# Alternating rooms for the first words of the Strassen blocks, and half of one weight sum moved from transfers to VectorE

## The chip, the cores and the metric

The kernel runs on one core of a Trainium2 chip. The time is the device time of one execution in microseconds (us). Three executions of the kernel before took 964.87, 967.33 and 967.99 us; the median is 967.33 us. One more execution was recorded by the hardware profiler and took 968.38 us, of which the first to the last instruction (the span) is 966.3 us; the other 2.1 us lie around it.

The engines are PE (TensorE, matrix products; PEld is its loading of the stationary operand), DVE (VectorE), ACT (ScalarE), POOL (GpSimd) and SP (SyncE, which here only issues loads). Sixteen DMA engines carry out the transfers. The tensors lie in HBM, the working tiles in SBUF, and the results of the matrix products in PSUM.

## The reference, cut to what matters

An encoder of two layers works on 256 tokens of width 1024 in float32. Each layer has an FFN, a mixer (mLSTM in layer 0, windowed attention in layer 1) and a second FFN, with a layer norm behind each. So there are six stages: FFN, mLSTM, FFN, FFN, attention, FFN. The change touches the four FFNs.

```python
D_MODEL, SEQ, DEPTH, D_FF = 1024, 256, 2, 2816
def swiglu(x, w_in, w_out):                 # w_in 1024 x 5632, w_out 2816 x 1024
    gu = x @ w_in
    g, u = gu[..., :D_FF], gu[..., D_FF:]
    return (jax.nn.silu(g) * u) @ w_out
# in each layer
x = layer_norm(ALPHA * x + 0.5 * swiglu(x, ffn_w_in[l, 0], ffn_w_out[l, 0]), ...)
y = mlstm_mixer(x, ...) if l % 2 == 0 else window_attention(x, ...)
x = layer_norm(ALPHA * x + y, ...)
x = layer_norm(ALPHA * x + 0.5 * swiglu(x, ffn_w_in[l, 1], ffn_w_out[l, 1]), ...)
```

## The kernel before

**Words and splits.** Every weight is used once, and it comes from HBM as a *word*: a tile of 128 x 1024 float32 (512 KB). A word is *split* into a high part, which ACT casts (`high`, tile `w_hi`), and a low part, the rest, which DVE subtracts (`low`, tile `w_lo`). A product of float32 accuracy is then three matmuls: high by high, high by low, low by high (`mm3`). PE needs both parts of a word; ten of each can be there at a time (`RING`), so the splits can run ahead of the products.

**Rooms.** A raw word lies in a *room*, a buffer of a pool, until its last low part or last sum is done (`drop`); then `load` issues the next word's transfer on SP. `w_raw` has 4 rooms and serves all stages. Within an FFN there are 2 spare rooms for the same words (`v_raw`, `V_RAW = 2`) and three kinds with 2 rooms each, `s_raw0` to `s_raw2`, for the Strassen blocks. The profile names a tile by its kind of word: `w_raw` (also in a spare room) or `s_raw`.

**A Strassen block** (`seven` in the plan, `seven` in `ffn`) makes 512 gate and 512 up columns of the FFN's hidden layer with seven products of blocks where eight would be due. The weights of a block are four quarters, of two words each: first (gate columns, upper rows; `b11`), second (up columns, upper rows; `b12`), third (gate columns, lower rows) and fourth (up columns, lower rows; `b22`). The words of `b11` are added to in place and split four times. The plan of one block, in the order in which the words are split, is:

- `s1`: the two words of `b11` as loaded. Behind each, `b11 += b12` on DVE, and `b12 +=` fourth quarter by an *accumulating transfer*: POOL issues a DMA that adds from HBM onto the tile (`sum`, line 272).
- the two words of the third quarter (`piece`), then one word of the output matrix (a *down* word).
- `s5`: `b11` again (now first + second). Behind each, `b11 += b22` on DVE. Then a second down word.
- `s6`: `b11` again. Behind each, `b11 +=` third quarter by an accumulating transfer.
- the two words of `b12` (second + fourth), the two of `b22`, two more down words, and last `b11` once more. This last pair of splits is called *s4* below. In the fourth block of an FFN the two late down words are left out.

So a block needs four sums on DVE and four accumulating transfers of 512 KB. A block's three kinds of rooms rotate: `TAGS[1 + (r + n) % 3]` gives the next block's `b11` the rooms of this block's `b12`, its `b12` those of `b22`, and its `b22` those of `b11`. An FFN has four blocks (`SEVENS = 4`), before them fourteen words and behind them six down words.

**The order in time.** Nothing is scheduled by the chip: each engine works off its instructions in the order in which the program wrote them, and waits at each for what it needs. The program decides the order while it is built, with a model of the engines' clocks (`Paced`). Within an FFN, after each matmul, `fill` writes a high part, a low part or a sum as soon as the model says that the engine is free and that the data have been there for 1 us (`SOON`). For a load the model counts `LANDING` and `LOADING`, for an accumulating transfer 8 us from its issue (`ADDING`). A product whose words are not yet split makes `take` write all splits of the plan up to them. The `turn` of a split gives the order in which PE takes it, where that differs from the order of splitting.

Between the products stand small steps on DVE and ACT. Two matter here: `end3` (a subtraction and a multiplication on DVE, 128 x 512, tile `e`), which makes the hidden values of the first 128 tokens, and `tr` behind it, four transposes by PE of that tile (`pw<-ident,e` in the profile), one down word later. The pair of `end3` is called *the e pair* below. The place where one block's late products meet the next block's first words is called *the border*.

Of the kernel before, what the change touches and what calls it, by code (L numbers as in the profile page):

```python
# [9 lines left out]
F32 = mybir.dt.float32  # L10
# [6 lines left out]
D = 1024  # L17
# [4 lines left out]
F = 2816  # L22
UNITS = F // 256
SEVENS = 4
RAW_BUFS = 4
S_RAW = 2
TAGS = ("w_raw", "s_raw0", "s_raw1", "s_raw2")
V_RAW = 2
RING = 10
PU = [2, 0, 1, 2, 1, 2, 1, 1, 0, 1, 2, 4]  # L30
QC = [2, 12, 20, 28, 32]
# [15 lines left out]
LANDING = 2200.0  # L47
LOADING = 1340.0
SECOND = 1250.0
ADDING = 8000.0  # L50


class Paced:
# [94 lines left out]
class Weights:  # L148
# [5 lines left out]
    def __init__(self, nc, pool, words, plan, after, turns):  # L154
# [4 lines left out]
        self.order, self.left = turns, set(range(len(plan)))  # L159
        self.todo = {tag: [i for i, w in enumerate(words) if w["tag"] == tag] for tag in TAGS}  # L160
        self.free = {"v_raw": 0, **{tag: 0 for tag in TAGS}, "w_raw": RAW_BUFS}
        self.spool, self.send, self.vbufs = None, 0, 0
# [13 lines left out]

    def open(self, pool, end, s_raw=S_RAW, v_raw=V_RAW):

# [84 lines left out]
    def sum(self):  # L263
        nc = self.nc
        _, w, v = self.sums.pop(0)
        t = self.raw[w]
        if isinstance(v, int):
            nc.vector.tensor_add(t, t, self.raw[v])
            self.drop(v)
            self.load()  # L270
        else:
            nc.gpsimd.dma_start(t.rearrange("p (k f) -> p k f", k=self.words[w]["k"]), v, accum_op=OP.add)  # L272
            nc.mark(t, max(nc.vec, nc.pe) + ADDING)

    def fill(self):

# [52 lines left out]
def trunk_kernel(ctx: ExitStack, tc: tile.TileContext, x, ffn_w_in, ffn_w_out, ln_g, ln_b, ml_w_in, ml_gate_b,  # L329
                 ml_norm_g, ml_w_out, at_w_in, at_sink, at_w_out, out):  # L330
    nc = Paced(tc.nc)
# [9 lines left out]
    words, plan, after = [], [], {}  # L341

    def word(src, k, tag="w_raw"):
        words.append(dict(src=src, k=k, tag=tag))
        return len(words) - 1

    def split_of(w, scale=None, needs=None):

        plan.append(dict(word=w, k=words[w]["k"], scale=scale, needs=needs, turn=len(plan)))
        return len(plan) - 1  # L350
# [4 lines left out]
    def two(w, r0, c0):  # L355
        return w[r0:r0 + 256, c0:c0 + 512].rearrange("(k p) f -> p k f", p=128)
# [12 lines left out]
    def rows(w, c, scale=None):  # L369
        piece(w[c * 128:(c + 1) * 128, :].rearrange("(k p) f -> p k f", p=128), 1, scale)  # L370

    def seven(w, c0, c1, n, downs):

        at = lambda r0, c: [two(w, r0 + 256 * j, c) for j in range(2)]
        b12, b11, b22 = ([word(x, 2, TAGS[1 + (r + n) % 3]) for x in at(*p)]
                         for r, p in ((1, (0, c1)), (0, (0, c0)), (2, (512, c1))))
        s1 = [split_of(w_) for w_ in b11]
        for a in at(512, c0):
            piece(a, 2)
        for j, a in enumerate(at(512, c1)):  # L380
            after[s1[j]] = [(b11[j], b12[j]), (b12[j], a)]
        downs(0)
        s5 = [split_of(w_, None, p) for w_, p in zip(b11, s1)]
        downs(1)
        for j in range(2):
            after[s5[j]] = [(b11[j], b22[j])]
        s6 = [split_of(w_, None, p) for w_, p in zip(b11, s5)]
        for j, a in enumerate(at(512, c0)):
            after[s6[j]] = [(b11[j], a)]
        plan[s6[0] - 1]["turn"] += 2.5  # L390
        [split_of(w_, None, p) for w_, p in zip(b12, s1)]
        for w_ in b22:
            split_of(w_)
        downs(2)
        downs(3)
        [split_of(w_, None, p) for w_, p in zip(b11, s6)]
        if n < SEVENS - 1:
            plan[-3]["turn"] += 2.5

    ends = {}  # L400
    for j, (kind, l, i, _) in enumerate(stages):
        if kind == "ffn":
            wi, wo = ffn_w_in[l, i], ffn_w_out[l, i]
            nth = iter(range(2 * UNITS))

            def down(n):
                for _ in range(n):
                    rows(wo, next(nth))

            for c0 in (0, F):  # L410
                for a in range(4):
                    wide(wi, a * 256, c0)
            for a in range(4):
                beside(wi, a * 256, 512, F + 512)
            down(2)
            for g in range(SEVENS):
                c0 = 768 + 512 * g
                seven(wi, c0, F + c0, g, lambda i_: down(1) if g < SEVENS - 1 or i_ < 2 else None)
            down(6)
        elif kind == "mlstm":  # L420
            for c0 in (1024, 1536):
                for a in range(4):
                    wide(ml_w_in[0], a * 256, c0)
            for c0 in range(0, 1024, 256):
                for a in range(2):
                    narrow(ml_w_in[0], a * 512, c0)
            for c0 in (2048, 2560):
                for a in range(4):
                    wide(ml_w_in[0], a * 256, c0)
            for c in range(8):  # L430
                rows(ml_w_out[0], c, (lambda c=c: gcol[:, c:c + 1]))
        else:
            for c0 in (1024, 0):
                for a in range(4):
                    wide(at_w_in[0], a * 256, c0)
            for c0 in (512, 768):
                for a in range(2):
                    narrow(at_w_in[0], a * 512, c0)
            for c in range(8):
                rows(at_w_out[0], c)  # L440
        ends[j] = len(words)
# [87 lines left out]
    def load_ln(room, l, n):  # L529
        t = []  # L530
        for name, w in (("g", ln_g), ("b", ln_b)):
            a = room("ln_" + name)
            src = w[l, n]
            nc.sync.dma_start(a, bass.AP(tensor=src.tensor, offset=src.offset, ap=[[0, 128], [1, D]]))
            t.append(a)
        return t
# [89 lines left out]
    def ffn(l, i, n, pending, last):  # L626
        with ExitStack() as ph:
            pool = ph.enter_context(tc.tile_pool(name="ffn", bufs=1))
# [140 lines left out]
            def down(n_):  # L769
                if not y:  # L770
                    y.extend([ybank() for _ in range(2)] for _ in range(2))
                for _ in range(n_):
                    c = done_[0]
                    w, = W.take(1)
                    for t in range(2):
                        for o in range(2):
                            mm3(y[t][o], pair(hT[c], A, tok(t)), pair(w, A, 0, slice(o * 512, o * 512 + 512)),
                                c == 0, False)
                    W.done()
                    done_[0] += 1  # L780
# [96 lines left out]
            def turn():  # L877
                p = wbank((128, 2, S))
                for t in range(2):
                    for k in range(2):  # L880
                        nc.tensor.transpose(p[:, k, tok(t)], hh[t][:, k * 128:(k + 1) * 128], ident)
                split_evac(hp, p)

            down(1)
            for g in range(SEVENS):
                turn = seven(g < SEVENS - 1, turn)
            if start:
                small_loads()
            nc.filler = None
            gb = load_ln(lambda name: pool.tile([128, D], F32, name=name, tag=TAGS[1 + SEVENS % 3], bufs=S_RAW), l, n)  # L890
            norm = [Norm(t, 2 * ALPHA, 4 * LN_EPS, gb, last) for t in range(2)]
            todo = list(zip(range(2 * UNITS - 6, 2 * UNITS), W.take_rows(6)))
            W.done(0)
# [510 lines left out]
    for j, (kind, l, i, n) in enumerate(stages):  # L1404
        last = j == len(stages) - 1
# [37 lines left out]
```

## Time and profile before

| what | value |
|---|---|
| three executions | 964.87, 967.33, 967.99 us |
| the profiled execution | 968.38 us, span 966.3 us |
| mean granted clock of TensorE | 0.984 |
| transfers | 208.53 MB in the span, mean 216 GB/s |
| busy share of PE, DVE, ACT, POOL | 95, 84, 59, 16% |
| `s_raw` loads on SP | 96, median 8.6 us from issue to landing |
| accumulating transfers on POOL | 64, median 6.8 us from issue to landing |

The page of the profile gives for each engine the busy time and the number of instructions. A row of a group of instructions ends in two parts behind bars: the busy time with the mean duration of one (ns), and the time that the engine stood idle just before them with what ended the idling. A row of the timeline gives start and length in us, engine, line, operation, output and inputs, the shape, the number of instructions that follow each other without a break, and in brackets the idle time before with what ended it. A row of the windows gives, for a stretch of the span, the busy time of each engine, the granted clock of TensorE (PEclk, 1.00 is full), the busy share of the sixteen DMA engines (which can come out a little above 1) and the GB/s. A row of the waits says who waited for whom: us in total, how often, and the longest.

### The profile page before, as it was taken

The numbers are of one execution on the slowest core, as the hardware profiler recorded it, in microseconds if no ns is written. First come the engines' busy times: TensorE is split into PE (matmuls) and PEld (weight loads), VectorE is DVE, ScalarE is ACT, GpSimd is POOL, SyncE is SP. The second block draws the span as 40 slices with busy tenths as digits, with TensorE's granted clock in tenths as the row PEclk, the third lists the DMA queues.
The fourth block names the chain that finished last, engine by engine and source line by source line (L and its number), as shares of the span: only waits on it lengthen the run. The fifth ranks groups of instructions, "written<-read, shape, count | busy, mean of one in ns | idle before, by whom it ended". The sixth has DMA issues, their size and how long they took to land.

```text
span 966.3 us, 12569 instructions
## 1 busy us (share of the span) xinstructions
PE 921.5 (95%) x4459; PEld 764.5 (79%) x4459; DVE 810.0 (84%) x969; ACT 568.3 (59%) x793; POOL 155.2 (16%) x194
## 2 busy tenths in 40 slices
PE   9998899799999999998989999898999999899896
PEld 7887778589988887887778888786888888788775
DVE  5889888787699798988897899887868889899776
ACT  5657565545765566656545676655459566666560
POOL 0012013022321010111011010110345301102010
PEclk9999999999999999998999999999999999999999
DMA  8998998545625979987659789876433387998941
GB/s 279 336 240 246 267 277 188 199 128 166 227 95 183 329 176 295 268 218 242 171 169 347 191 263 301 258 176 200 141 139 131 96 279 236 253 268 223 280 109 44
DMA packets 100702, 208.53 MB, mean 216 GB/s; under 512 B 6904, under 2 KB 21264, under 8 KB 100640
## 3 DMA queue, kind: packets, MB, share of 16 engines
q1 hardware_dynamic: 82368, 173.04, 51.2%
q0 software_dynamic: 17696, 33.65, 20.6%
q10 hardware_dynamic: 576, 1.05, 0.3%
q8 instruction: 35, 0.57, 0.2%
q14 instruction: 27, 0.22, 0.1%
HBM read 206.65 MB, written 1.05 MB: 215 GB/s over the span
## 4 chain that ended last, share of the span: by engine, by line
PE 43%; DVE 19%; DMA 15%; issue 15%; ACT 4%; POOL 3%; SPq 0%; DVEq 0%; POOLq 0%; ACTq 0%
PE pw L139 28%; PE py L139 15%; DMA s_raw<-in_ffn_w_in_dram 11%; DVE w_lo L139 9%; ACT w_hi L139 3%; DVE s_raw L139 3%; DVE e L139 2%; POOL s_raw L272 2%; DMA w_raw<-in_ffn_w_out_dram 1%; DMA w_raw<-in_ml_w_in_dram 1%; DMA w_raw<-in_ffn_w_in_dram 1%; DVE h_lo L139 1%; DMA w_raw<-in_at_w_in_dram 1%; DVE x L139 1%; DVE h L139 1%
## 5 line engine op out<-in xcount | busy, mean ns | idle before, releaser
L139 DVE TENSOR_TENSOR w_lo<-w_raw,w_hi 128x1024 fp32r<-128x1024 f32 (+1 forms) x213 | 253.8, 1219 | 28.9 <-ACT w_hi L139 26.8
L139 DVE TENSOR_TENSOR w_lo<-s_raw,w_hi 128x1024 fp32r<-128x1024 f32 x192 | 227.5, 1219 | 52.1 <-ACT w_hi L139 47.8
L139 ACT CAST w_hi<-w_raw 128x1024 fp32r<-128x1024 f32 (+1 forms) x213 | 216.1, 1046 | 69.4 <-PE py L139 22.1
L139 ACT CAST w_hi<-s_raw 128x1024 fp32r<-128x1024 f32 x192 | 191.9, 1051 | 79.4 <-DMA s_raw<-in_ffn_w_in_dram 50.0
L139 PE MATMUL pw<-w_hi,xT_hi 128*128 128x512 f32 x480 | 193.5, 404 | 1.7 <-ACT w_hi L139 1.7
L139 PE MATMUL pw<-w_hi,xT_lo 128*128 128x512 f32 x480 | 189.1, 395 | 0.8 <-DVE xT_lo L139 0.8
L139 PE MATMUL pw<-w_lo,xT_hi 128*128 128x512 f32 x480 | 188.9, 395 | 0.4 <-DVE w_lo L139 0.4
L272 POOL DMA_DIRECT2D s_raw<-in_ffn_w_in_dram x64 | 77.7, 1232 | 519.4 <-ACT w_hi L139 158.5
L139 PE MATMUL py<-w_hi,h_lo 128*128 128x512 f32 x349 | 138.2, 396 | 6.2 <-DVE h_lo L139 6.2
L139 PE MATMUL py<-w_hi,h_hi 128*128 128x512 f32 x349 | 138.6, 397 | 3.4 <-ACT h_hi L139 3.4
L139 PE MATMUL py<-w_lo,h_hi 128*128 128x512 f32 x349 | 138.2, 396 | 2.5 <-DVE w_lo L139 2.5
L139 PEld LDWEIGHTS pw<-w_hi,xT_lo 128*128 128x128 f32 x480 | 91.6, 191 | 21.2 <-DVE xT_lo L139 1.3
L139 PEld LDWEIGHTS pw<-w_hi,xT_hi 128*128 128x128 f32 x480 | 91.6, 191 | 19.6 <-ACT w_hi L139 2.1
L139 PEld LDWEIGHTS pw<-w_lo,xT_hi 128*128 128x128 f32 x480 | 91.9, 191 | 19.0 <-DVE w_lo L139 1.2
L139 PE MATMUL pw<-w_hi,S_hi 128*128 128x512 f32 x256 | 99.6, 389 | 0.0
L139 PE MATMUL pw<-w_lo,S_hi 128*128 128x512 f32 x256 | 99.6, 389 | 0.0
L139 PE MATMUL pw<-w_hi,S_lo 128*128 128x512 f32 x256 | 99.6, 389 | 0.0
L139 PEld LDWEIGHTS py<-w_hi,h_lo 128*128 128x128 f32 x349 | 66.5, 191 | 21.6 <-DVE h_lo L139 7.9
L139 PEld LDWEIGHTS py<-w_lo,h_hi 128*128 128x128 f32 x349 | 66.4, 190 | 19.7 <-DVE w_lo L139 6.4
L139 PEld LDWEIGHTS py<-w_hi,h_hi 128*128 128x128 f32 x349 | 66.7, 191 | 17.8 <-ACT h_hi L139 4.3
L139 DVE TENSOR_TENSOR s_raw<-s_raw,s_raw 128x1024 f32<-128x1024 f32 x64 | 78.3, 1224 | 2.5 <-DMA s_raw<-in_ffn_w_in_dram 0.8
L139 ACT COPY e<-pw 128x512 f32<-128x512 f32 x48 | 28.2, 587 | 61.7 <-PE pw L139 61.7
(205 smaller groups left out, 1157.0 us busy)
## 6 DMA issues: line engine op xcount, KB each, us to landing
s_raw<-in_ffn_w_in_dram SPq DMA_DIRECT2D x96, 512.0 KB, 8.6
w_raw<-in_ffn_w_out_dram SPq DMA_DIRECT2D x88, 512.0 KB, 7.0
w_raw<-in_ffn_w_in_dram SPq DMA_DIRECT2D x64, 512.0 KB, 4.9
s_raw<-in_ffn_w_in_dram POOLq DMA_DIRECT2D x64, 512.0 KB, 6.8
w_raw<-in_ml_w_in_dram SPq DMA_DIRECT2D x24, 512.0 KB, 4.6
w_raw<-in_ffn_w_in_dram SPq DMA_DIRECT2D x32, 256.0 KB, 3.4
w_raw<-in_at_w_in_dram SPq DMA_DIRECT2D x12, 512.0 KB, 4.6
w_raw<-in_ml_w_out_dram SPq DMA_DIRECT2D x8, 512.0 KB, 4.0
```

Of the source, the lines that this page charges most:

```text
L139: r = f(out, *args, **kw)
L272: nc.gpsimd.dma_start(t.rearrange("p (k f) -> p k f", k=self.words[w]["k"]), v, accum_op=OP.add)
```

## The change

Five things change.

1. A fourth kind of room, `s_raw3`, comes in (two rooms), and the spare rooms `v_raw` go from 2 to 1, so an FFN has 13 rooms where it had 12. The rooms no longer rotate: `b12` always has `s_raw1`, `b22` always `s_raw2`, and `b11` has `s_raw0` in even blocks and `s_raw3` in odd ones. The layer norm's two vectors go into `s_raw0`.
2. The last pair s4 of a block is split behind the next block's `s1` (`late`). The order in which PE takes the words stays.
3. The second down word is split behind `s6`, not between `s5` and `s6`.
4. In every FFN but the first (`both` is `j == 0`), for one of the two words of `b12`, the sum of second and fourth quarter is `b12 += b22` on DVE behind `s5`, and the accumulating transfer for it is dropped. For the other word, and in the first FFN for both, the transfer stays. These are 12 transfers fewer of 64 and 12 DVE sums more.
5. In the model of the clocks an accumulating transfer now also takes up the transfers' time: 2500 ns each (`SHARE`), so loads issued behind it count as landing later.

```diff
-TAGS = ("w_raw", "s_raw0", "s_raw1", "s_raw2")
-V_RAW = 2
+TAGS = ("w_raw", "s_raw0", "s_raw1", "s_raw2", "s_raw3")
+V_RAW = 1
...
+SHARE = 2500.0
...
             nc.gpsimd.dma_start(t.rearrange("p (k f) -> p k f", k=self.words[w]["k"]), v, accum_op=OP.add)
-            nc.mark(t, max(nc.vec, nc.pe) + ADDING)
+            now = max(nc.vec, nc.pe)
+            nc.dma = max(nc.dma, now + LANDING) + SHARE
+            nc.mark(t, now + ADDING)
...
-    def seven(w, c0, c1, n, downs):
-        at = lambda r0, c: [two(w, r0 + 256 * j, c) for j in range(2)]
-        b12, b11, b22 = ([word(x, 2, TAGS[1 + (r + n) % 3]) for x in at(*p)]
-                         for r, p in ((1, (0, c1)), (0, (0, c0)), (2, (512, c1))))
+    def seven(w, c0, c1, n, down, late, both):
+        def at(r0, c):
+            return [two(w, r0 + 256 * j, c) for j in range(2)]
+        b12, b11, b22 = ([word(x, 2, TAGS[r]) for x in at(*p)]
+                         for r, p in ((2, (0, c1)), (4 if n % 2 else 1, (0, c0)), (3, (512, c1))))
+        first = len(plan)
+        used = iter(range(99))
+        def turn(n_):
+            for p in plan[-n_:]:
+                p["turn"] = first + 0.01 * next(used)
         s1 = [split_of(w_) for w_ in b11]
+        turn(2)
+        for j, a in enumerate(at(512, c1)):
+            after[s1[j]] = [(b11[j], b12[j])] + [(b12[j], a)] * (j or both)
+        late()
         for a in at(512, c0):
             piece(a, 2)
-        for j, a in enumerate(at(512, c1)):
-            after[s1[j]] = [(b11[j], b12[j]), (b12[j], a)]
-        downs(0)
+        turn(2)
+        down()
+        turn(1)
         s5 = [split_of(w_, None, p) for w_, p in zip(b11, s1)]
-        downs(1)
+        turn(2)
         for j in range(2):
-            after[s5[j]] = [(b11[j], b22[j])]
+            after[s5[j]] = [(b11[j], b22[j])] + [(b12[j], b22[j])] * (not (j or both))
+        full = n < SEVENS - 1
         s6 = [split_of(w_, None, p) for w_, p in zip(b11, s5)]
+        turn(2)
         for j, a in enumerate(at(512, c0)):
             after[s6[j]] = [(b11[j], a)]
-        plan[s6[0] - 1]["turn"] += 2.5
-        [split_of(w_, None, p) for w_, p in zip(b12, s1)]
+        down()
+        turn(1)
+        [split_of(w_, None, p) for w_, p in zip(b12, (s1[0] if both else s5[0], s1[1]))]
+        turn(2)
         for w_ in b22:
             split_of(w_)
-        downs(2)
-        downs(3)
-        [split_of(w_, None, p) for w_, p in zip(b11, s6)]
-        if n < SEVENS - 1:
-            plan[-3]["turn"] += 2.5
+        turn(2)
+        if full:
+            down()
+            turn(1)
+        at4 = [next(used) for _ in range(2)]
+        if full:
+            down()
+            turn(1)
+        def last():
+            for j in range(2):
+                split_of(b11[j], None, s6[j])
+                plan[-1]["turn"] = first + 0.01 * at4[j]
+        return last
...
+            late = lambda: None
             for g in range(SEVENS):
                 c0 = 768 + 512 * g
-                seven(wi, c0, F + c0, g, lambda i_: down(1) if g < SEVENS - 1 or i_ < 2 else None)
+                late = seven(wi, c0, F + c0, g, lambda: down(1), late, j == 0)
+            late()
             down(6)
...
-            gb = load_ln(lambda name: pool.tile([128, D], F32, name=name, tag=TAGS[1 + SEVENS % 3], bufs=S_RAW), l, n)
+            gb = load_ln(lambda name: pool.tile([128, D], F32, name=name, tag=TAGS[1], bufs=S_RAW), l, n)
```

## The prediction

> **What bounds the kernel now.** I read the page first, then the waits of PE, then the timeline where PE waits, then windows over blocks.
>
> ```profile
> span 966.3 us, 12569 instructions
> ...
> PE 921.5 (95%) x4459; PEld 764.5 (79%) x4459; DVE 810.0 (84%) x969; ACT 568.3 (59%) x793; POOL 155.2 (16%) x194
> ```
>
> PE is the bound with 95%, so only its idle time and its slow time can be won. The waits of PE, over the whole span and then over the blocks of the four FFNs in turn (40 to 180 us, 340 to 480, 530 to 665, 805 to 966):
>
> ```profile
> PE pw L139 <- DVE e L139: 20.6, 10, 3.0
> PE pw L139 <- ACT w_hi L139: 1.7, 1, 1.7
> PE py L139 <- DVE w_lo L139: 2.7, 10, 0.9
> ...
> PE pw L139 <- DVE e L139: 7.6, 3, 2.8
> PE pw L139 <- DVE e L139: 3.9, 2, 3.0
> PE pw L139 <- DVE e L139: 3.1, 2, 2.8
> PE pw L139 <- DVE e L139: 6.0, 3, 2.9
> ```
>
> PE hardly waits for split weights (2.7 us for low parts). It waits ten times, 20.6 us, for the e pair: the transposes `tr` at the borders of blocks. Why the pair is late, at the first border (timelines of POOL, SP, DVE, ACT and PE, put in order of time; between them how long the two accumulating transfers took to land, each asked of its own window):
>
> ```profile
> 59.49 2.44 POOL L272 DMA_DIRECT2D s_raw<-in_ffn_w_in_dram  x2 [10.30 <-DVE w_lo L139]
> ...
> DMA to landing us min/median/max: 5.7/5.7/5.7
> ...
> DMA to landing us min/median/max: 10.9/10.9/10.9
> ...
> 61.49 3.78 SPq L105 DMA_DIRECT2D s_raw<-in_ffn_w_in_dram  x4
> 66.03 1.48 SPq L105 DMA_DIRECT2D w_raw<-in_ffn_w_out_dram  x2
> ...
> 67.06 1.22 DVE L139 TENSOR_TENSOR w_lo<-s_raw,w_hi 128x1024 fp32r<-128x1024 f32 x1
> 68.25 0.69 DVE L139 TENSOR_TENSOR e<-e,pw 128x512 f32<-128x512 f32 x1
> ...
> 71.56 2.95 ACT L139 CAST w_hi<-s_raw 128x1024 fp32r<-128x1024 f32 x3 [5.21 <-DMA s_raw<-in_ffn_w_in_dram]
> ...
> 72.65 2.36 DVE L139 TENSOR_TENSOR w_lo<-s_raw,w_hi 128x1024 fp32r<-128x1024 f32 x2 [3.72 <-ACT w_hi L139]
> 74.93 0.69 DVE L139 TENSOR_TENSOR e<-pw,e 128x512 f32<-128x512 f32 x1
> 75.65 0.69 DVE L139 TENSOR_TENSOR e<-e,e 128x512 f32<-128x512 f32 x1
> ...
> 76.49 0.63 PE L139 MATMUL pw<-ident,e 128*128 128x128 f32 x4 [2.84 <-DVE e L139]
> ```
>
> The second transfer for s4 is issued at 60.6 (second of the pair at 59.49) and lands 10.9 us later, at 71.5, beside a burst of loads from 61.49 on. ACT stands 5.21 us before its high part, DVE 3.72 us before its low part, and the e pair, which has all it needs, is written behind that low part. In DVE's order three low parts stand ahead of the pair: 67.06 is the first word of s4, 72.65 (x2) the second of s4 and the first of the next block's `s1`.
>
> The idle stretches cost a second time. The windows behind four of them, one more of the gaps, and then whole blocks:
>
> ```profile
> 143.40:146.90 3.50, 3.50 (x11) 2.91 (x12) 3.50 (x4) 1.53 (x2) 1.20 (x1) 0.51 0.67 242
> 440.30:447.30 7.00, 6.05 (x17) 4.93 (x18) 5.99 (x7) 2.48 (x3) 2.41 (x2) 0.51 0.85 172
> 628.10:631.60 3.50, 3.50 (x11) 2.75 (x10) 3.47 (x5) 2.48 (x3) 1.14 (x1) 0.51 0.90 145
> 904.60:908.10 3.50, 2.97 (x10) 2.58 (x11) 3.46 (x5) 1.85 (x3) 0.98 (x2) 0.51 0.77 170
> ...
> 840.26 0.41 PE L139 MATMUL pw<-ident,e 128*128 128x128 f32 x2 [2.44 <-DVE e L139]
> ...
> 76.90:110.40 33.50, 31.05 (x143) 25.47 (x141) 29.53 (x30) 21.25 (x25) 4.84 (x4) 1.00 0.91 252
> 376.70:407.60 30.90, 30.90 (x144) 25.59 (x142) 28.84 (x29) 20.30 (x24) 4.80 (x4) 1.00 0.91 255
> 563.30:594.20 30.90, 30.90 (x143) 25.59 (x142) 29.01 (x29) 20.31 (x24) 4.82 (x4) 1.00 0.93 260
> ```
>
> In 17.5 us the clock is at 0.51, so 17.5 x 0.49 = 8.6 us are lost. A block of the first FFN takes 33.5 us from border to border, one without a wait 30.9. **The ceiling** is 20.6 + 1.7 + 8.6 = 30.9 us. The two borders without a wait show that the same products need no wait.
>
> **The change part by part.**
>
> *s4 split behind the next `s1`.* Nothing is added; two low parts and two high parts change places with two. Now three low parts stand ahead of the e pair; if as many stand there after, they are two of `s1` and the first of s4, whose transfer landed in 5.7 us. The late second word comes behind the pair and is not missed yet: at the first border it lands at 71.5, plus a high part of 1.05 and a low part of 1.22 makes 73.8, and PE, which without the wait would do `tr` at 76.49 - 2.84 = 73.65 and then the first word of s4, 12 matmuls for two words at the blocks' pace, asks for the second word later than that. For the two low parts of `s1` to run early, their word must be there: in its own room it can be loaded a block ahead, where before it came with the burst at 61.49. Queued behind s4's waiting high part on ACT are the third quarter's high parts and the next casts of evacuations; DVE's queue is what counts, and there the pair is ahead. Bounds of the rest of a wait per border: 0 (the pair is ahead), and 2.84 - 1.22 = 1.6 us (the order against the pair stays as it was, and only the transfer starts one low part earlier, below). I take 0.5, since the blocks of 30.9 us show borders at 0; for 12 borders 6.0 us stay.
>
> *Second down word behind `s6`.* One low part (1.22 us) less ahead of the accumulating transfer, so that starts by as much earlier. Against it, `s6` has one split less to cover its sum on DVE. Rows of the sum and of POOL's issue:
>
> ```profile
> L139 DVE TENSOR_TENSOR s_raw<-s_raw,s_raw 128x1024 f32<-128x1024 f32 x64 | 78.3, 1224 | 2.5 <-DMA s_raw<-in_ffn_w_in_dram 0.8
> L272 POOL DMA_DIRECT2D s_raw<-in_ffn_w_in_dram x64 | 77.7, 1232 | 519.4 <-ACT w_hi L139 158.5
> ```
>
> The second word's low part and sum lie between and cover a cast of 1.05 us. Taken at 0, bounds -1.2 and +1.2 per block, inside the 0.5 above.
>
> *Sums on VectorE for transfers.* Removed: 12 x 1.23 us of issue on POOL (519.4 us idle ahead of it: nothing) and 12 of 64 transfers. Their engine time:
>
> ```profile
> q1 hardware_dynamic: 82368, 173.04, 51.2%
> q0 software_dynamic: 17696, 33.65, 20.6%
> ```
>
> 20.6% of 966.3 us over 64 is 3.1 us each (a load of 512 KB: 51.2% over 173.04 MB, 1.5 us), 37 us of transfers less, which nobody waits for by themselves; it shows in landing times. Added: 12 x 1.224 = 14.7 us on DVE. In a block without waits DVE has 28.84 to 29.01 of 30.9 us; with one sum it has 30.1 to 30.2, so 0.7 us of cover is left, and behind the sum stand the low parts of `s5` and `s6`. Bounds 0 (covered) and 14.7; nearest is the room of 0.7 us, so near 0: I take 2.0.
>
> *Rooms.* Loads keep their number but for their order. At the start of an FFN all `s_raw` rooms fill at once, now eight and not six:
>
> ```profile
> 23.68 0.60 SPq L105 DMA_DIRECT2D w_raw<-in_ffn_w_out_dram  x1
> 24.33 4.80 SPq L105 DMA_DIRECT2D s_raw<-in_ffn_w_in_dram  x6
> 29.24 0.67 SPq L105 DMA_DIRECT2D w_raw<-in_ffn_w_out_dram  x1
> ...
> 40.01 1.05 ACT L139 CAST w_hi<-w_raw 128x1024 fp32r<-128x1024 f32 x1 [1.53 <-DMA w_raw<-in_ffn_w_out_dram]
> ...
> 187.41 1.05 ACT L139 CAST w_hi<-w_raw 128x1024 fp32r<-128x1024 f32 x1 [3.90 <-DMA w_raw<-in_ml_w_in_dram]
> ```
>
> The load at 29.24 moves behind two more, 2 x 1.5 = 3.0 us, and with a spare room less the one at 23.68 comes behind the `s_raw` loads too. ACT already waited 1.53 us for it. Bounds 0 and 4 x 3.0 = 12; PE had no wait of this kind in the windows above, so I take 1.0, in the first FFN. At the end of an FFN a room less for the six down words can hold the next stage's first load back by a word; ACT waits there today (3.90 us). Bounds -2 and +4 (one word of 1.3 us at three boundaries); taken at 0, since the next stage never used the spare rooms.
>
> *`SHARE`.* No instruction; loads count 2.5 us later per accumulating transfer, so splits of late words are written later. This is what keeps the order above; 0 by itself.
>
> **Sum.** 30.9 - 6.0 - 2.0 - 1.0 = 21.9 us off the profiled execution's 968.4 us gives 946.5. The median shown is 1 us below that execution, so I say **946**.
>
> **The clock.** The half clock begins as the gap ends, after gaps of at most 3.0 us, in four of the seven large ones (rival 1). The Trainium skill, "TensorE: Matmul & The Clock Gate", Part 1, says that the clock halves after at least one idle window of about 3.4 us. By that rule no gap here would have done it, and the 8.6 us would stay whatever the gaps do: 955. The rows differ from the rule, so I count the clock with the gaps.
>
> **The rivals.**
>
> *1. The pair stays behind the late word.* The model still writes both words of s4 ahead of the pair. Seven gaps are large: three in the first FFN (7.6), 3.0, 2.8, 2.44 and 2.9; the other three make 20.6 - 18.7 = 1.9 us. Then the large ones lose 1.2 us each (8.5) and the small ones go; half of the clock's 8.6 comes back. 968.4 - 8.5 - 1.9 - 4.3 + 3.0 = 957. For: the model put 8 us on a transfer of 10.9. Against: three splits ahead, now of other words.
>
> *2. VectorE becomes the bound in three FFNs.* All 14.7 us show: 946.5 + 12.7 = 959. For: 0.7 us of cover. Against: DVE's waits of 3.72 us go.
>
> *3. The next block's sum takes the place of the late word (slower).* `b11 += b12` of the next block is now due before s4, and `b12`'s room comes free only in the burst at 61.49; its second load goes at about 62.6. If the model writes this sum ahead of the pair and the load takes 11.4 us, the longest of any `s_raw` transfer, it lands at 74.0, sum 75.2, pair 76.6, where 73.65 was due: 2.9 us at each of 12 borders (35 us), with 1.2 us of clock each (8.6 over seven): 968.4 - 30.9 + 35 + 15 + 3 = 990. It decides from 1.6 us per border with the clock, a landing 10.1 us after issue; the middle is 979. For: loads in the burst share with two transfers. Against: median landing of 8.6 us, and `SHARE`.
>
> ```profile
> s_raw<-in_ffn_w_in_dram SPq DMA_DIRECT2D x96, 512.0 KB, 8.6
> ...
> DMA to landing us min/median/max: 5.6/8.1/11.4
> ```
>
> *4. Nothing moves.* Gaps go and come back elsewhere: 967.
>
> *5. The clock does not come back:* 955, above.
>
> **How the numbers follow.** Forecast 0.55 (938 to 954), rival 1 0.15, rival 2 0.10, rival 5 0.05, rival 3 0.11, rival 4 0.04. Range 936 to 965: all 30.9 won and 1.5 us of better stage ends, up to rivals 1 and 2 with 6 us; it leaves out rivals 3 and 4 and the tails, 0.2. A change of 0.3% (2.9 us) is about what a measurement of this kernel tells from none. Faster 0.85, within 0.3% 0.04, slower 0.11. The forecast's own range is 938 to 954.
>
> **What the profile after would show.** PE's wait for `e` under 7 us and no PEclk of 0.51 behind a border (right) or 10 us and more (rival 1, 3). DVE at a border: two low parts of `s1`, one of s4, the pair, the second of s4. ACT's wait for `s_raw` by transfers below half. 52 accumulating transfers and 76 sums on DVE; blocks of the later FFNs at 31 us (right) or 32 and more with DVE at 97% (rival 2). DVE waiting for a transfer before a sum would be rival 3. A PE wait for low parts near the 40th us of the span or at the ends of FFNs would show the rooms' price. The prediction is wrong if the model's new order puts another late word ahead of the pair.

## The result, and the profile after

Over 20 executions the kernel after takes 970.40 us in the median (964.77 to 974.08). The kernel before, over 20 executions beside them, takes 968.99 us (964.87 to 975.92). The ratio is 1.0009 with a 95% interval of 0.9991 to 1.0028: no difference that this measurement can tell. The forecast of 946 us and its range of 936 to 965 us missed. The profiled execution of after took 970.03 us, with a span of 968.3 us and a mean granted clock of 0.983.

First the page of after: the span, the engines, the queue of the accumulating transfers (packets, MB, share of the sixteen DMA engines), the chain by engine, and the groups of the sums and of the accumulating transfers.

```profile
span 968.3 us, 12517 instructions
...
PE 922.8 (95%) x4459; PEld 765.4 (79%) x4459; DVE 823.1 (85%) x981; ACT 568.6 (59%) x793; POOL 140.6 (15%) x182
...
q0 software_dynamic: 14432, 27.35, 17.0%
...
DVE 37%; PE 26%; DMA 24%; issue 8%; ACT 4%; POOL 1%; SPq 0%; DVEq 0%; ACTq 0%; POOLq 0%
...
L140 DVE TENSOR_TENSOR s_raw<-s_raw,s_raw 128x1024 f32<-128x1024 f32 x76 | 92.0, 1224 | 16.5 <-DMA s_raw<-in_ffn_w_in_dram 14.4
...
L273 POOL DMA_DIRECT2D s_raw<-in_ffn_w_in_dram x52 | 62.9, 1213 | 535.7 <-ACT w_hi L140 222.0
```

The counts are those forecast: 52 accumulating transfers and 76 sums, and the share of the DMA engines that these transfers take falls from 20.6 to 17.0%. PE is as busy as before (922.8 against 921.5 us). What moved is the chain that ended last. The same row of the page of before was:

```profile
PE 43%; DVE 19%; DMA 15%; issue 15%; ACT 4%; POOL 3%; SPq 0%; DVEq 0%; POOLq 0%; ACTq 0%
```

VectorE's part of the chain went from 19 to 37%, the transfers' from 15 to 24%, and PE's fell from 43 to 26%. In the sums' row the idle time ahead of them, spent on a transfer, went from 0.8 to 14.4 us.

The waits of PE in after (us in total, how often, the longest), and below them one row each of the waits of DVE and of ACT:

```profile
PE pw L140 <- DVE e L140: 21.7, 16, 3.7
PE py L140 <- DVE h_lo L140: 5.3, 6, 2.0
PE py L140 <- ACT h_hi L140: 4.5, 2, 3.6
PE pw L140 <- DVE w_lo L140: 3.7, 2, 3.2
```

```profile
DVE s_raw L140 <- DMA s_raw<-in_ffn_w_in_dram: 14.4, 13, 2.2
```

```profile
ACT w_hi L140 <- DMA s_raw<-in_ffn_w_in_dram: 18.4, 12, 2.3
```

In before, ACT's row was:

```profile
ACT w_hi L139 <- DMA s_raw<-in_ffn_w_in_dram: 50.0, 19, 5.3
```

So ACT no longer stands before the late word (50.0 us became 18.4), as forecast. Its waiting has moved, though: for the sums of VectorE ahead of its casts it waited 29.3 us in before (20 times) and waits 65.9 us in after (30 times). And PE's wait for the e pair is as large as it was (20.6 us ten times, now 21.7 us sixteen times), and VectorE now waits for transfers ahead of its sums.

The timeline of DVE over the first border of the second FFN shows both. The last row is PE's, from its own timeline:

```profile
361.19 1.22 DVE L140 TENSOR_TENSOR w_lo<-s_raw,w_hi 128x1024 fp32r<-128x1024 f32 x1
363.79 1.23 DVE L140 TENSOR_TENSOR s_raw<-s_raw,s_raw 128x1024 f32<-128x1024 f32 x1 [1.38 <-DMA s_raw<-in_ffn_w_in_dram]
364.93 1.22 DVE L140 TENSOR_TENSOR w_lo<-s_raw,w_hi 128x1024 fp32r<-128x1024 f32 x1
366.58 1.23 DVE L140 TENSOR_TENSOR s_raw<-s_raw,s_raw 128x1024 f32<-128x1024 f32 x1 [0.43 <-DMA s_raw<-in_ffn_w_in_dram]
367.73 0.68 DVE L140 TENSOR_TENSOR e<-e,pw 128x512 f32<-128x512 f32 x1
368.33 2.35 DVE L140 TENSOR_TENSOR w_lo<-s_raw,w_hi 128x1024 fp32r<-128x1024 f32 x2
370.60 0.68 DVE L140 TENSOR_TENSOR e<-pw,e 128x512 f32<-128x512 f32 x1
371.31 0.69 DVE L140 TENSOR_TENSOR e<-e,e 128x512 f32<-128x512 f32 x1
```

```profile
372.15 1.09 PE L140 MATMUL pw<-ident,e 128*128 128x128 f32 x4 [2.50 <-DVE e L140]
```

The low parts at 361.19 and 364.93 are those of the next block's `s1`. Each is followed by a sum `b11 += b12` of that next block, and VectorE stands 1.38 and 0.43 us before them for the loads of `b12`. Then come both low parts of s4 (368.33, x2), and only then the e pair at 370.60, for which PE idles 2.50 us. The row at 367.73 is an earlier step between the products. The timelines at the other borders show the same at ten of the twelve: all four low parts and both sums stand ahead of the pair. At the first two borders of the first FFN one and three low parts stand there.

Windows over five blocks of the later FFNs, from border to border. The columns are those of the prediction's windows:

```profile
372.20:405.90 33.70, 32.41 (x140) 26.56 (x141) 30.88 (x31) 21.36 (x25) 3.58 (x3) 0.96 0.79 234
405.90:438.60 32.70, 31.08 (x141) 25.50 (x141) 30.88 (x31) 21.26 (x25) 3.61 (x3) 1.00 0.82 241
595.90:627.60 31.70, 31.08 (x141) 25.51 (x141) 30.88 (x31) 21.32 (x25) 3.61 (x3) 1.00 0.82 249
843.70:878.50 34.80, 33.81 (x141) 27.62 (x141) 30.98 (x31) 21.34 (x25) 3.59 (x3) 0.92 0.76 228
878.50:910.90 32.40, 31.03 (x141) 25.48 (x141) 30.84 (x31) 21.26 (x25) 3.61 (x3) 1.00 0.82 244
```

A block has 31 instructions of VectorE and 30.8 to 31.0 us of its work, and it takes 31.7 to 34.8 us. VectorE has as much to do in it as PE has in a block without a wait (30.9 us). By stage, from the last transposes ahead of an FFN's blocks (`pw<-ident,hh`) to the `tr` of its fourth block, read from the starts of those rows in the timeline of PE (us):

| FFN | before | after |
|---|---|---|
| first | 124.6 | 126.8 |
| second | 122.0 | 123.5 |
| third | 120.0 | 122.6 |
| fourth | 124.8 | 125.2 |

No FFN got shorter: together they take 6.8 us more. Something else got shorter, by 7.9 us: the stretch from the end of the first FFN's blocks to the start of the second's, with the mLSTM in it, takes 177.1 us in before and 169.2 in after. In before (176 to 350 us) PE waits there for 5.2 us, and its clock is low behind these waits:

```profile
PE py L139 <- DVE h_lo L139: 2.0, 1, 2.0
PE py L139 <- ACT h_hi L139: 1.7, 1, 1.7
PE py L139 <- DVE w_lo L139: 1.5, 4, 0.9
...
186.00:200.00 14.00, 10.31 (x34) 7.72 (x33) 9.59 (x12) 3.63 (x4) 1.55 (x1) 0.76 0.51 173
```

In after, 0.6 us of such waits are left. SP issues the mLSTM's first four loads together there, from 174.70 us on; in before two go out at 176.15 and the next at 179.70. No run tests this gain by itself. It takes rooms and order together: the stretch is 179.6 us with the rooms alone and 176.4 us with the order alone (both runs below).

### The profile page after: what moved, and what is told of

Its sections match the earlier page's. It is cut to its first block, busy times and chain, and to the rows that moved or that the text cites. A ratio compares the mean times of both kernels' runs of the same rounds, so it can differ in the third digit from the quotient of the medians.

```text
span 968.3 us, 12517 instructions
## 1 busy us (share of the span) xinstructions
PE 922.8 (95%) x4459; PEld 765.4 (79%) x4459; DVE 823.1 (85%) x981; ACT 568.6 (59%) x793; POOL 140.6 (15%) x182
## 4 chain that ended last, share of the span: by engine, by line
DVE 37%; PE 26%; DMA 24%; issue 8%; ACT 4%; POOL 1%; SPq 0%; DVEq 0%; ACTq 0%; POOLq 0%
DVE w_lo L140 21%; PE pw L140 17%; DMA s_raw<-in_ffn_w_in_dram 15%; PE py L140 8%; DMA w_raw<-in_ffn_w_in_dram 4%; DVE e L140 4%; DVE s_raw L140 4%; DMA w_raw<-in_ffn_w_out_dram 3%; ACT w_hi L140 2%; DVE h_lo L140 2%; DVE x L140 2%; DVE stats L140 1%; DMA w_raw<-in_at_w_in_dram 1%; DMA w_raw<-in_ml_w_in_dram 1%; DVE h L140 1%
## 5 line engine op out<-in xcount | busy, mean ns | idle before, releaser
L140 ACT CAST w_hi<-s_raw 128x1024 fp32r<-128x1024 f32 x192 | 194.3, 1049 | 88.4 <-DVE s_raw L140 65.9
L273 POOL DMA_DIRECT2D s_raw<-in_ffn_w_in_dram x52 | 62.9, 1213 | 535.7 <-ACT w_hi L140 222.0
L140 DVE TENSOR_TENSOR s_raw<-s_raw,s_raw 128x1024 f32<-128x1024 f32 x76 | 92.0, 1224 | 16.5 <-DMA s_raw<-in_ffn_w_in_dram 14.4
L140 PEld LDWEIGHTS py<-w_hi,h_lo 128*128 128x128 f32 x349 | 66.3, 190 | 21.7 <-DVE h_lo L140 7.8
L140 PEld LDWEIGHTS py<-w_hi,h_hi 128*128 128x128 f32 x349 | 66.5, 191 | 19.1 <-ACT h_hi L140 5.3
L140 ACT CAST h_hi<-pw 128x512 fp32r<-128x512 f32 x44 | 25.8, 588 | 66.6 <-PE pw L140 66.5
```

Of the source, the lines that this page charges most:

```text
L140: r = f(out, *args, **kw)
```

## The experiments

Two theories stood against each other. V says that VectorE's own time is what the gain went into: the 12 sums leave it no slack. Q says that it is the place in VectorE's queue: the next block's sums and low parts stand ahead of the e pair and wait for loads. A third reading, D, puts it down to the data, that is when transfers and loads land. Each experiment has its theories' numbers as they were recorded.

### VectorE's time

**All by transfer.** After, with item 4 of the change taken back:

```diff
-                late = seven(wi, c0, F + c0, g, lambda: down(1), late, j == 0)
+                late = seven(wi, c0, F + c0, g, lambda: down(1), late, True)
```

> The kernel after, with the sum of second and fourth quarter by accumulating transfers for both words in all FFNs (64 transfers and 64 sums on VectorE as before); rooms and order as after. Theory V: 8 to 14 us faster than after. Theory Q: the next block's sums still stand ahead of the pair, so within 4 us of after, PE's wait for e 17 to 27 us.

Measured: 948.48 us, 0.9781 of before (0.9753 to 0.9808). That is 22 us less than after, for 12 sums of 1.22 us (14.7 us). Of 19.1 us between the two profiled spans (968.3 and 949.2), 10.6 are PE's wait for `e`, which is now 11.1 us, and 7.0 are PE's busy time (915.8 against 922.8 us, at a mean granted clock of 0.987 against 0.983). The three FFNs that lose their sums take 118.1, 117.2 and 117.9 us, so 5.4, 5.4 and 7.2 us less, where four sums of each are 4.9 us; the first FFN takes 127.0, as in after. The row of PE's wait, and two windows over blocks:

```profile
PE pw L140 <- DVE e L140: 11.1, 9, 2.3
```

```profile
371.40:403.70 32.30, 31.07 (x140) 25.46 (x141) 29.78 (x30) 21.46 (x25) 4.81 (x4) 1.00 0.94 266
587.60:618.70 31.10, 31.07 (x141) 25.53 (x141) 29.84 (x30) 21.57 (x25) 4.82 (x4) 1.00 0.95 270
```

With 29.8 us of VectorE's work a block takes down to 31.1 us. V's direction held, its size was too small. Q's range, within 4 us of after, was missed.

**The sum left out.** Is it the sum on VectorE that costs, or is there a gain of the 12 transfers that only the sum hides? Here neither is made. This kernel leaves out a part of the computation: fourth quarter is not added to second for one of the two words of each block of the three FFNs.

```diff
-            after[s5[j]] = [(b11[j], b22[j])] + [(b12[j], b22[j])] * (not (j or both))
+            after[s5[j]] = [(b11[j], b22[j])]
...
-        [split_of(w_, None, p) for w_, p in zip(b12, (s1[0] if both else s5[0], s1[1]))]
+        [split_of(w_, None, p) for w_, p in zip(b12, s1)]
```

> The kernel after, with the 12 sums on VectorE left out altogether (in the three later FFNs one word of b12 goes unsummed, so that part of the computation is missing): neither a transfer nor an instruction. Theory V (each added sum lengthens VectorE's full queue in a block): as fast as with all sums by transfer, 942 to 951 us. If the order and the rooms of after, with fewer transfers, are what costs: 962 to 972 us.

Measured: 948.14 us, 0.9782 (0.9756 to 0.9808), the same as with all 64 transfers. So 12 accumulating transfers fewer bring nothing.

**All by transfer, and VectorE kept busy.** The kernel with all transfers, and behind `s5` of each block of the three later FFNs one instruction on VectorE that changes nothing, the maximum of a word of `b22` with itself:

```diff
+        if v == "idle":
+            nc.vector.tensor_max(t, t, t)
...
-            after[s5[j]] = [(b11[j], b22[j])] + [(b12[j], b22[j])] * (not (j or both))
+            after[s5[j]] = [(b11[j], b22[j])] + [(b22[j], "idle")] * (idle and not j)
```

> All sums by transfer (the kernel of e3), and where after has its sum on VectorE, an instruction of the same size that changes nothing (the larger of b22 and b22, in place) in each block of the three later FFNs: 12 more instructions of 1.2 us on VectorE, nothing else. Theory V: the 20 us that e3 won against after are lost again, 963 to 973 us. If not VectorE's time but the sum's waits count (on b12 or on what the transfer left): 946 to 954 us.

Measured: 972.01 us, 1.0018 (0.9993 to 1.0043), so the whole of the loss is back, with the 12 transfers kept. The group of these instructions, PE's wait for the pair, and a block:

```profile
L140 DVE TENSOR_TENSOR s_raw<-s_raw 128x1024 f32<-128x1024 f32 x12 | 14.7, 1226 | 0.4
```

```profile
PE pw L140 <- DVE e L140: 24.6, 16, 4.2
```

```profile
574.60:606.90 32.30, 31.06 (x142) 25.48 (x141) 30.80 (x31) 21.27 (x25) 4.82 (x4) 1.00 0.83 240
```

They wait 0.4 us in all for their word, so it is not a wait of the sum's own, nor what it computes: one more instruction of 1.23 us on VectorE per block costs the same.

### Each part alone, on the kernel before

**The rooms alone.** Items 1 without 2 to 5:

```diff
-TAGS = ("w_raw", "s_raw0", "s_raw1", "s_raw2")
-V_RAW = 2
+TAGS = ("w_raw", "s_raw0", "s_raw1", "s_raw2", "s_raw3")
+V_RAW = 1
...
-        b12, b11, b22 = ([word(x, 2, TAGS[1 + (r + n) % 3]) for x in at(*p)]
-                         for r, p in ((1, (0, c1)), (0, (0, c0)), (2, (512, c1))))
+        b12, b11, b22 = ([word(x, 2, TAGS[r]) for x in at(*p)]
+                         for r, p in ((2, (0, c1)), (4 if n % 2 else 1, (0, c0)), (3, (512, c1))))
```

> The kernel before with the new rooms alone (fourth kind of room, fixed rooms for b12 and b22, one spare room; order, sums and model as before). Theory Q: s4's second word stays ahead of the pair, so PE's wait for e stays between 14 and 24 us and the time within 4 us of before. If the burst of loads in s4's way is the cause and the alternating rooms thin it out (theory D in its mild form): second transfers land in 8 us and not 11, PE's wait for e under 10 us, 950 to 958 us.

Measured: 978.60 us, 1.0100 (1.0071 to 1.0128). The second transfers for s4 do not land earlier (10.8, 11.2 and 11.8 us at the borders of the first FFN), so D in its mild form is out. The pair is as late as Q said: PE waits 23.7 us for it, ten times. But the time is 10 us longer, not within 4 us as Q had it. The trace shows 3.7 us more of PE's wait for `h_hi` (7.1 against 3.4 us) and a lower clock (0.977) beside it; why the rooms alone cost this is open.

**The order alone.** Items 2, 3 and 5, all sums by transfer, with the rotating rooms and two spare rooms of before (the diff is that of the change without `TAGS`, `V_RAW` and the fixed rooms, and with `late, True)` as above).

> The new order of splitting and the new model of transfers, with the rooms of before (three rotating kinds, two spare rooms) and all sums by transfer. If the order alone does what e3 shows (theory Q): 945 to 955 us. If it needs the rooms, since b11 of the next block must be there early for its split to stand ahead of s4: VectorE and ScalarE wait for s_raw loads at the borders, 960 to 975 us.

Measured: 993.14 us, 1.0232 (1.0196 to 1.0268), slower than either theory said. The rows of PE's waits and of ACT's:

```profile
PE pw L140 <- DVE e L140: 22.7, 15, 2.9
PE pw L140 <- DVE w_lo L140: 11.8, 7, 3.2
```

```profile
ACT w_hi L140 <- DMA s_raw<-in_ffn_w_in_dram: 58.7, 27, 5.3
```

ACT waits for loads even more than in before (50.0 us), and low parts are late too. This fits the plan, by which the next `s1` cannot be there early with rotating rooms; no run tests that step by itself. Rooms and order each lose alone (+1.0%, +2.3%) and together, without the sums, win 2.2%: the one needs the other.

**The sums alone.** Item 4 on the kernel before:

```diff
-            after[s1[j]] = [(b11[j], b12[j]), (b12[j], a)]
+            after[s1[j]] = [(b11[j], b12[j])] + [(b12[j], a)] * (j or both)
...
-            after[s5[j]] = [(b11[j], b22[j])]
+            after[s5[j]] = [(b11[j], b22[j])] + [(b12[j], b22[j])] * (not (j or both))
```

> The kernel before with the 12 sums on VectorE in place of 12 transfers, and nothing else of the change. In the kernel before VectorE stands 3 to 4 us before s4's second low part at 7 borders, so the added 1.2 us per block can hide there: within 4 us of before (theory V with that cover). If VectorE's time counts even there: 8 to 15 us slower. If the transfers saved let the late words land earlier: 5 us or more faster.

Measured: 978.88 us, 1.0094 (1.0069 to 1.0120), some 10 us slower. The pair is as late as before, and the low parts come later:

```profile
PE pw L139 <- DVE e L139: 20.4, 12, 2.8
PE py L139 <- DVE w_lo L139: 7.2, 14, 1.6
...
PE pw L139 <- DVE w_lo L139: 5.3, 6, 1.1
```

In the kernel before, too, there was little cover for them: some 10 of their 14.7 us show.

### The queue at the border

**A longer transfer in the model of before.** Only the model's number for an accumulating transfer is changed, so that the late word is written behind the pair:

```diff
-ADDING = 8000.0
+ADDING = 12000.0
```

> The kernel before, with one number changed: the model counts 12 us instead of 8 us for an accumulating transfer (ADDING), so that both splits of s4 are written behind the e pair in VectorE's queue; no transfer, room or sum changes. If what stands ahead of the pair in VectorE's queue is the cause of the border waits (theory Q): PE's wait for e falls from 20.6 us to under 7, no half clock behind a border, 943 to 952 us. If the words of s4 are late by their transfers whatever the order (theory D): the wait passes to low or high parts of s4, PE idles as long, 963 to 970 us.

Measured: 993.70 us, 1.0254 (1.0226 to 1.0282), slower than either theory said. The pair is on time: no row for `e` is left. But now PE waits 48.5 us for low parts:

```profile
PE pw L139 <- DVE w_lo L139: 39.0, 22, 2.4
PE py L139 <- DVE w_lo L139: 9.5, 13, 2.0
```

To put the pair first is not enough: in the old order of the plan other words come late in its place. I read it so that the late word holds back what stands behind it in the plan; no run takes that apart further.

**After, with the next block's sums held back.** The same constant, and `b12`'s loads count as landing 8 us later, so that the model writes `b11 += b12` later:

```diff
-ADDING = 8000.0
+ADDING = 12000.0
...
+            if tag == TAGS[2]:
+                nc.mark(t, nc.dma + 8000.0)
```

> The kernel after, with two numbers of the model changed: a load of b12 counts 8 us longer, and an accumulating transfer 12 us, so that the next block's sums b11 += b12 and both splits of s4 are written behind the e pair. Theory Q: the pair is no longer held up, PE's wait for e from 21.7 us to under 7, 943 to 955 us. If the added sums fill VectorE in the last three FFNs (theory V): waits for e go, but PE waits 8 us or more for low parts there, 957 to 966 us. Theory D: 965 to 972 us.

Measured: 963.79 us, 0.9943 (0.9919 to 0.9967). The waits of PE:

```profile
PE pw L140 <- DVE w_lo L140: 12.2, 6, 2.4
PE py L140 <- DVE w_lo L140: 10.4, 16, 2.3
...
PE pw L140 <- DVE e L140: 0.4, 1, 0.4
```

The pair is on time here as well (0.4 us of wait, 21.7 in after), by a change of nothing but the order in which the program writes. So the order of VectorE's queue made it late. Most of what that wins is lost to low parts, 22.6 us against 3.9 in after, and the time lies in V's range.

**All by transfer, sums held back 4 us.** Without the added sums, and with less delay:

```diff
+            if tag == TAGS[2]:
+                nc.mark(t, nc.dma + 4000.0)
...
-                late = seven(wi, c0, F + c0, g, lambda: down(1), late, j == 0)
+                late = seven(wi, c0, F + c0, g, lambda: down(1), late, True)
```

> All sums by transfer (e3), and a load of b12 counts 4 us longer in the model, so that the next block's two sums b11 += b12 are written behind the e pair or next to it. Theory Q: PE's wait for e, 11.1 us in e3, falls under 4, and with VectorE having room nothing else comes up: 935 to 946 us. If what is put behind the pair is missed elsewhere: waits for low parts of 8 us and more, 946 to 955 us.

Measured: 936.38 us, 0.9665 (0.9642 to 0.9688), faster than both kernels. PE's waits, a block, and VectorE at a border of the second FFN:

```profile
PE pw L140 <- DVE w_lo L140: 2.9, 3, 2.4
PE pw L140 <- DVE e L140: 2.3, 5, 0.7
```

```profile
395.30:426.10 30.80, 30.80 (x141) 25.52 (x140) 29.55 (x30) 21.45 (x25) 4.80 (x5) 1.00 0.91 263
```

```profile
387.27 4.62 DVE L140 TENSOR_TENSOR w_lo<-s_raw,w_hi 128x1024 fp32r<-128x1024 f32 x4
391.81 0.68 DVE L140 TENSOR_TENSOR e<-e,pw 128x512 f32<-128x512 f32 x1
392.41 2.35 DVE L140 TENSOR_TENSOR s_raw<-s_raw,s_raw 128x1024 f32<-128x1024 f32 x2
394.68 0.68 DVE L140 TENSOR_TENSOR e<-pw,e 128x512 f32<-128x512 f32 x1
```

All four low parts run in one stretch, the two sums come behind them without a wait, and the pair follows. The sums still stand ahead of the pair at this border; what is gone is VectorE's wait for the loads of `b12`, which was 10.8 us in all with all transfers and no delay and is in none of the rows of 0.6 us and more here. PE is busy for the whole of the window: 30.8 of 30.8 us. The four FFNs take 121.3, 115.0, 115.7 and 115.8 us. One block stays long, the first of the first FFN, with 36.1 us.

**The same delay with the added sums, and other delays.** After with the two lines of 4 us alone:

> The kernel after, with its 12 sums on VectorE, and a load of b12 counting 4 us longer in the model, as in e8; it differs from e8 in the added sums alone (and the 12 transfers). Theory V: VectorE is full with them, so what no longer waits at the e pair waits elsewhere; 15 to 22 us above e8: 951 to 958 us. If the added sums cost only since they stood ahead of the pair (theory Q alone): 934 to 942 us.

Measured: 950.16 us, 0.9801 (0.9778 to 0.9823). That is 1 us below V's range and far above Q's. PE waits for the pair twelve times, 9.8 us in all. So the added sums cost 13.8 us in this order (950.16 - 936.38), close to their 14.7 us of VectorE's time, and the delay of 4 us brings 20 us to after and 12 us to the kernel with all transfers. The delay itself was varied in the latter, `2000.0` and `8000.0` in place of `4000.0`:

> As e8, but a load of b12 counts 2 us longer; in the three later FFNs one of the two sums is then written ahead of the e pair and one behind. Theory Q: between e3 (948) and e8 (936), 938 to 945 us, with PE's wait for e between 3 and 10 us.

> As e8, but a load of b12 counts 8 us longer, not 4, so the next block's sums come behind the e pair and two or more low parts later. If 4 us is enough and more only makes b11's second split late: 937 to 948 us, waits of PE for low parts of s5 and s6 words. If the pair still gains: 931 to 936 us.

Measured: 936.67 us, 0.9663 (0.9640 to 0.9686), with 2 us, and 944.20 us, 0.9736 (0.9711 to 0.9762), with 8 us. Between 2 and 4 us nothing changes, so 2 us did better than expected. With 8 us the time lies in the first range, but not for the reason given: PE's waits for low parts are small (1.3 and 2.9 us), and the blocks of the four FFNs together are 4.5 us shorter than with 4 us. The stretch between the first FFN's blocks and the second's takes 178.5 us against 170.2, and that is the loss.

## Why the prediction was wrong, point by point

**The ceiling.** Near, in part by luck: 30.9 us off 968.4 would be 937.5, and the best kernel of the study, which removes nearly all of the border waits, takes 936.4. But in its profile 23.6 us of the gain lie in the blocks, and 6.9 us in the stretch between the first two FFNs, where the ceiling counted nothing. The clock came back in good part with the gaps (0.984 to 0.991 in the mean, some 7 us), so rival 5 is out. In after the gaps stayed, and so did the clock (0.983).

**"s4 split behind the next `s1`" and "Rooms".** The total of the two came out near the forecast: without the sums on VectorE 948.5 us, where the forecast without its 2.0 us for them would be 944.5. That is luck in part. Of the 17.1 us between the two profiled spans (966.3 and 949.2) only 11.1 lie in the blocks, to which the prediction put nearly all of its 23.9; 8.2 lie in the stretch between the first two FFNs, where it took the effect of the rooms at 0; the rest lost 2.2.

The step on the order failed. The prediction took it that three low parts would stand ahead of the pair, "two of `s1` and the first of s4". In after all four low parts and both sums `b11 += b12` stand there at ten of twelve borders, and VectorE waits for the loads of `b12` between them. That is the mechanism of rival 3 at a smaller size: 21.7 us of PE's wait in all, where rival 3 had 35. Of PE's wait for the pair 6.0 us were to stay; without the sums on VectorE it is 11.1 us. In the kernel with all transfers, to take VectorE's waits away brought 12 us (948.48 to 936.38). The first FFN, which has no added sum, takes 126.8 us in after and 127.0 with all transfers, and 121.3 with the delay.

That a word of s4 behind the pair "is not missed yet" failed as well, at the first border. There the pair is ahead of s4, and PE waits for the first low part of s4, which stands behind the second low part of the next `s1` and a sum; its clock is at 0.51 from 78.00 to 84.90:

```profile
78.74 0.80 PE L140 MATMUL pw<-w_lo,xT_hi 128*128 128x512 f32 x1 [3.18 <-DVE w_lo L140]
```

The rooms were priced 1.0 us between 0 and 12; alone they cost 10 us, and what they cost beside the order no run here tells. The wait for low parts near 40 us that would have shown it is not there; the largest wait for a low part is the one above.

**"Sums on VectorE for transfers: 2.0".** This is the step that decided. The bounds 0 and 14.7 were worked out, and the value was put near 0 because "0.7 us of cover is left". That cover came from two windows with 28.84 and 29.01 us of VectorE's work, which hold x29 instructions. A block has 30: the window of the first FFN in the prediction had x30 and 29.53 us, the second block of the second FFN in before (407.60 to 441.60) has x30 and 29.46 us, and after shows 30.9 us with x31. So against 30.9 us of PE the cover was 0 and not 0.7. Even that would have cost nothing if the totals decided, since 30.9 us fit into 30.9. They do not: VectorE works in order and also waits in a block, and in the block from 405.90 it is idle for 1.8 of 32.7 us, of which 1.3 are one wait for `b12`. Measured, the sums cost 22 us here (970.40 against 948.48), 13.8 us with the delay and 10 us on the kernel before. That it is more than 14.7 us in after fits the clock: 0.983 of 968.3 us is a loss of 16.5 us, and 0.987 of 949.2 us one of 12.3. Rival 2 had the mechanism, at 12.7 us and a chance of 0.10.

**"37 us of transfers less, which nobody waits for by themselves".** Right: without sums and transfers 948.14, with the transfers 948.48.

**"Second down word behind `s6`" and "`SHARE`".** Taken at 0. No run tested either by itself.

**The wait that should shrink.** ACT's wait for `s_raw` by transfers fell below half as said (50.0 to 18.4 us), and this did not show in the time, since the pair now stood behind other words.

**The signs.** Those named for rivals 2 and 3 both came: blocks of 31.7 to 34.8 us with VectorE nearly full, and VectorE waiting 14.4 us for transfers before sums. So did the last one, another late word ahead of the pair.

**The total.** It looks like rival 4, nothing moves, and it is not: a gain of some 20 us and a loss of some 22 us lie on top of each other.

## What to carry to other kernels

Before work is moved onto an engine, count that engine's instructions over one whole period and set its busy time against the period that you are aiming at, not the present one; here a window one instruction short showed 0.7 us of slack where there was none. Totals that just fit are not cover either: 12 sums cost nearly their whole time (13.8 of 14.7 us) in the best order tried. Where an engine works in order, look at what the program writes ahead of the instruction that the critical engine waits for, and whether each of those has its data: here a delay of 2 to 4 us in the model's dates for one kind of load was worth more (12 to 20 us) than 12 transfers (0). Try parts of a change alone and together, since two that lose alone can win together.

## What the runs showed of the hardware

**Gaps of 2.0 to 2.5 us can halve the clock.** Two gaps of PE in after, from its timeline, and the windows behind them:

```profile
145.56 0.63 PE L140 MATMUL pw<-ident,e 128*128 128x128 f32 x4 [2.02 <-DVE e L140]
```

```profile
146.40:149.80 3.40, 3.40 (x10) 2.62 (x9) 3.11 (x4) 2.30 (x3) 0.00 (x0) 0.50 0.98 255
371.70:375.10 3.40, 2.95 (x9) 2.58 (x10) 2.65 (x4) 1.82 (x3) 0.00 (x0) 0.50 1.08 308
```

In the first case the gap ends at 145.56, and the clock is at half speed for 3.4 us from 146.40 on. In the second it is so from 371.70 on, in a gap that began at 372.15 - 2.50 = 369.65, so 2.0 us into it. Not every gap does it: in before PE ran on at full clock after the 2.84 us at 76.49 (the window 76.90 to 110.40 has 1.00). The Trainium skill, "TensorE: Matmul & The Clock Gate", Part 1, gives a free-running window of about 3.4 us; the length of the half clock agrees with it, but its rule that an idle window of that length comes first does not hold here. That the window runs freely could be why gaps of one length differ; no run here tests it.

**An engine in order needs slack of more than nothing.** With the same order (the delay of 4 us), three blocks of the later FFNs with 30 instructions and 29.6 us of VectorE's work took 30.9 us each, all of it busy time of PE. Three blocks with 31 instructions and 30.7 to 30.8 us of work took 31.1 to 31.6 us, though VectorE was not full in them. One instruction in 31 decided.
